# Forming the low part of every fourth weight pair with ScalarE and an accumulating transfer in an fp32 decoder trunk

## Chip, cores and metric

The kernel runs on one core of a Trainium2 chip. The metric is the device time of one execution in microseconds (us). The core's engines are TensorE (PE, with its weight loads as PEld), VectorE (DVE), ScalarE (ACT), GpSimd (POOL) and SyncE (SP); SP, ACT and POOL each have a queue from which they issue transfers to the core's 16 DMA engines.

## Reference

The kernel computes a two-layer decoder trunk in float32 for 256 positions of width 2048. Cut to what matters here:

```python
for i in range(DEPTH):                      # DEPTH = 2
    h = rms_norm(x, attn_norm_w[i])
    if i < N_A_LAYERS:
        x = x + mixer_a(h, a_w_qkv[i], a_w_o[i])
    else:
        k_blocks, v_blocks = shared_kv_blocks(x, kv_norm_w, b_w_kv, positions)
        x = x + mixer_b(h, b_w_q[j], b_w_o[j], k_blocks, v_blocks, positions)
    x = x + conv_ffn(rms_norm(x, ffn_norm_w[i]), ffn_w_up[i], ffn_conv_w[i], ffn_conv_b[i], ffn_w_down[i])
    gate = jax.nn.sigmoid(rms_norm(x, ple_norm_w[i]) @ ple_w_gate[i])
    x = x + gate * (p[i] @ ple_w_proj[i])
return rms_norm(x, final_norm_w)
```

Every `@` is a product of the 256 positions with a weight matrix of some 2048 to 11264 columns. All weights together are read once, 435 MB, and these products make up nearly all of the work.

## The kernel before

**Split operands.** TensorE multiplies in a rounded float32 format (float32r). To keep float32 accuracy, each operand is split into a high part, the value rounded to that format, and a low part, what is left: w = hi + lo. A product is then formed from three of the four partial products. For the activations the two parts stand side by side in one tile of 128 x 512 (`h`, `g`, `o` in the trace: 256 columns high, 256 low).

**The weights' way.** `weights` (L199) is a generator that feeds all large products. It walks over one strip of 512 output columns in blocks of 128 rows of the weight matrix. SyncE loads four blocks at a time (1 MB, L209) into a tile `raw`, of which there are four (`NRAW`). For each two of these blocks, a *pair*, ScalarE copies them to `whi` with rounding (L217), and VectorE subtracts, `wlo = raw - whi` (L218). There are four tiles `whi` and four `wlo` (`NWSP`), used in turn. These two instructions are issued at a raised priority (`tc.high_priority(offset=AHEAD)`), so that the scheduler puts them ahead of other work on ScalarE and VectorE as far as free buffers allow. There are 824 pairs; the first eight, while the activations are still coming in, are loaded two blocks at a time (`fine`).

**The products.** `strip_t` (L235) keeps the weights stationary: for a pair and four groups of 128 columns it issues eight matmuls with `whi` over all 512 activation columns (L246) and then eight with `wlo` over the 256 high columns (L249). `strip_1` (L252, lines L262 to L264) does the same with three shorter matmuls for each block and column group, the low one first; it serves the embedding gate and its projection. `strip_v` (L267, L276 to L278) keeps the activations stationary, for the values of the attention. `steps` (L221) sets the order of the groups: in the middle of a strip a whole pair is one group; the first pair of a strip goes output by output; the last pair (`tail=2`, in the very last strips `tail=4`: two pairs) is held back and also goes output by output, so that the four outputs become ready one after the other. The accumulators are five PSUM banks with the tag `acc`.

**Around the products.** `evac` (L281) brings an accumulator to SBUF (a ScalarE copy `c`, L283, and VectorE operations), followed in `ffn` by the convolution (L519 to L521), the gate (L531) and the split of the result (`split`, L142). The order of instructions on each engine is fixed when the program is built, by the scheduler from priorities and its own estimates; each engine then works its list in order and waits on semaphores.

Of the kernel before, what the change touches and what calls it, by code (L numbers as in the profile page):

```python
# [14 lines left out]
AF = mybir.ActivationFunctionType  # L15
OP = mybir.AluOpType
# [57 lines left out]
def tile_trunk(ctx, tc, xT_d, pT_d, pos_d, vec_d, cst_d, csb_d, wqkv, wo_a, wkv, wq_b, wo_b, wup, wdn, wpg, wpp, out_d):  # L74
    nc = tc.nc
# [9 lines left out]
    def nm(s):  # L85
        uid[0] += 1
        return f"{s}_{uid[0]}"
# [14 lines left out]
    f32 = lambda ap: ap.bitcast(F32)  # L102
# [43 lines left out]
    class Norm:  # L146
# [25 lines left out]
        def done(self, column=False):  # L172
# [23 lines left out]
            nc.vector.tensor_copy(rc[:, 0:4:2], pc[:, 0:4:2])  # L196
            return r, rc

    def weights(W, s, n, fine=False, before=lambda k0: None, base=0):  # L199

        size = 2 if fine else RAW
        for k0 in range(0, n, size):
            w = min(size, n - k0)
            raw = wraw.tile([P, RAW, 512], F32, tag="raw", name=nm("raw"))
            j = (base + k0) % W.shape[3]
            one = fine and k0 == 0
            for q in range(w) if one else (slice(0, w),):
                src = slice(j + q, j + q + 1) if one else slice(j, j + w)
                nc.sync.dma_start(raw[:, slice(q, q + 1) if one else q, :], W[s, (base + k0) // W.shape[3], :, src, :])  # L209
            for i in range(0, w, 2):  # L210
                hi = wsp.tile([P, 2, 512], F32R, tag="hi", name=nm("whi"))
                lo = wsp.tile([P, 2, 512], F32R, tag="lo", name=nm("wlo"))
                before(k0 + i)
                with tc.high_priority(offset=AHEAD):
                    for c in (slice(0, 1), slice(1, 2)) if one else (slice(0, 2),):
                        r = raw[:, i + c.start : i + c.stop]
                        nc.scalar.activation(hi[:, c], r, AF.Copy)  # L217
                        nc.vector.tensor_tensor(lo[:, c], r, f32(hi[:, c]), op=OP.subtract)  # L218
                yield k0 + i, hi, lo

    def steps(it, n, outs, tail=2, begin=True):  # L221
# [13 lines left out]
    def strip_t(W, s, xs, fine=False, before=lambda k0: None, base=0):  # L235

        n = len(xs)
        ps = [None] * 4
        for group in steps(weights(W, s, n, fine, before, base), n, 4, begin=not fine):
            if fine and group[0][0] == 0:  # L240
                group.sort(key=lambda g: g[0])
            for k, o, hi, lo in group:
                if k == 0:
                    ps[o] = bank("acc", "acc")
                c = slice(o * P, (o + 1) * P)
                nc.tensor.matmul(ps[o], hi[:, c], xs[k], start=k == 0, stop=False)  # L246
            for k, o, hi, lo in group:
                c = slice(o * P, (o + 1) * P)
                nc.tensor.matmul(ps[o][:, S:], lo[:, c], xs[k][:, :S], start=False, stop=k == n - 1)  # L249
        return ps  # L250

    def strip_1(W, s, xs, tail=2, two=None):  # L252

        n = len(xs)
        ps = [None] * 2
        a = dict(skip_group_check=True)
        for k, o, hi, lo in (g for group in steps(weights(W, s, n), n, 4, tail) for g in group):
            if k == 0 and o % 2 == 0:
                ps[o // 2] = two[:, o // 2, :] if two is not None else bank("acc", "acc")
            c = slice(o * P, (o + 1) * P)  # L260
            d = ps[o // 2][:, (o % 2) * S : (o % 2 + 1) * S]
            nc.tensor.matmul(d, lo[:, c], xs[k][:, :S], start=k == 0 and o % 2 == 0, stop=False, **a)  # L262
            nc.tensor.matmul(d, hi[:, c], xs[k][:, S:], start=False, stop=False, **a)  # L263
            nc.tensor.matmul(d, hi[:, c], xs[k][:, :S], start=False, stop=k == n - 1, **a)  # L264
        return [ps[o // 2][:, (o % 2) * S : (o % 2 + 1) * S] for o in range(4)]

    def strip_v(W, s, xs):  # L267

        n = len(xs)
        ps = [None] * 2  # L270
        for k, t, hi, lo in (g for group in steps(weights(W, s, n), n, 2) for g in group):
            if k == 0:
                ps[t] = bank("accv", "acc")
            xh = xs[k][:, t * P : (t + 1) * P]
            xl = xs[k][:, S + t * P : S + (t + 1) * P]
            nc.tensor.matmul(ps[t], xl, hi, start=k == 0, stop=False)  # L276
            nc.tensor.matmul(ps[t], xh, lo, start=False, stop=False)  # L277
            nc.tensor.matmul(ps[t], xh, hi, start=False, stop=k == n - 1)  # L278
        return ps
# [439 lines left out]
```

## Time and profile before

| what | value |
|---|---|
| median of 2 runs | 2398.07 us (2397.55 to 2398.58) |
| the profiled execution | 2398.34 us, span 2396.5 us |
| granted TensorE clock | 0.998 |
| GpSimd | 3.6 us busy, 6 instructions |
| HBM read and written | 435.55 MB and 2.10 MB, 183 GB/s over the span |
| SyncE's 1 MB weight loads | 404, median 4.8 us from issue to landing |

The span is the time from the first to the last instruction of the profiled execution. A group's row in the profile gives line, engine, operation, tile written and tiles read, shape and count; behind the bar stand the busy time, the mean duration of one in ns, the idle time just before, and what ended it. A row of waits reads "who waits <- for whom: us in total, times, longest". A row of the order of time gives the start in us, the duration, the engine and line, the operation, and in brackets the idle time before it. Several like instructions in a row are merged (x8).

### The profile page before, as it was taken

The page shows a single profiled execution, that of the slowest core. Times are in us where ns is not written, and L with a number is a line of the kernel's source. Part 1 is how long each engine was busy: PE and PEld are TensorE (multiplying, and loading weights), DVE is VectorE, ACT ScalarE, POOL GpSimd, SP SyncE. Part 2 cuts the span into 40 slices and gives each one's busy share as a digit, 9 for nine tenths or more (in the row PEclk, how much of TensorE's full clock was granted, in tenths as well). Part 3 has the DMA queues.
Part 4 walks back from the last instruction along what each step waited for, and adds up shares of the span by engine and source line. Part 5 has one row for each costly group of instructions (what it writes and reads, how often), then busy time and mean ns, then how long its engine had stood idle before and what let it go on. Part 6 is the DMA issues. An engine that isn't in the chain of part 4 may idle for free.

```text
span 2396.5 us, 35018 instructions
## 1 busy us (share of the span) xinstructions
PE 2373.7 (99%) x13914; PEld 2091.5 (87%) x13914; DVE 1651.2 (69%) x2654; ACT 1277.0 (53%) x1845; POOL 3.6 (0%) x6
## 2 busy tenths in 40 slices
PE   8999999999999999999999999999999999999997
PEld 7888888888888888888998888888888888888897
DVE  8555557777765577766778875777776557776665
ACT  6555545655643455654555444565564345565453
POOL 0000000000000000000000000000000000000000
PEclk9999999999999999999999999999999999999999
DMA  7444455555555555555455544555555555555542
GB/s 279 167 167 166 168 176 198 185 185 193 192 183 188 193 179 191 192 193 183 173 190 187 175 150 169 187 192 183 190 190 193 185 185 192 192 184 188 184 168 106
DMA packets 64004, 439.92 MB, mean 184 GB/s; under 512 B 7232, under 2 KB 7392, under 8 KB 12128
## 3 DMA queue, kind: packets, MB, share of 16 engines
q1 hardware_dynamic: 62352, 435.19, 51.6%
q8 instruction: 109, 1.79, 0.3%
q10 hardware_dynamic: 1488, 2.49, 0.3%
q14 instruction: 55, 0.45, 0.1%
HBM read 435.55 MB, written 2.10 MB: 183 GB/s over the span
## 4 chain that ended last, share of the span: by engine, by line
PE 98%; DVE 1%; ACT 0%; DMA 0%; issue 0%; DVEq 0%; SPq 0%; ACTq 0%
PE acc L246 54%; PE acc L249 27%; PE acc L264 2%; PE acc L262 2%; PE acc L263 2%; PE accv L277 2%; PE accv L276 2%; PE accv L278 2%; PE po L306 1%; PE two L262 0%; PE two L264 0%; PE two L263 0%; PE two L364 0%; PE two L448 0%; PE po L307 0%; DMA x<-in_xT 0%
## 5 line engine op out<-in xcount | busy, mean ns | idle before, releaser
L218 DVE TENSOR_TENSOR wlo<-raw,whi 128x1024 fp32r<-128x1024 f32 (+1 forms) x825 | 1008.1, 1222 | 669.3 <-ACT whi L217 662.3
L217 ACT ACTIVATE whi<-raw 128x1024 fp32r<-128x1024 f32 (+1 forms) x825 | 871.8, 1057 | 872.4 <-PE acc L246 694.9
L246 PE MATMUL acc<-h,whi 128*128 128x512 f32 x3712 | 993.3, 394 | 9.0 <-DVE h L136 9.0
L246 PEld LDWEIGHTS acc<-h,whi 128*128 128x128 f32 x3712 | 643.0, 189 | 99.3 <-DVE h L136 9.0
L249 PEld LDWEIGHTS acc<-h,wlo 128*128 128x128 f32 x3712 | 554.4, 190 | 67.9
L249 PE MATMUL acc<-h,wlo 128*128 128x256 f32 x3712 | 573.2, 282 | 0.0
L246 PE MATMUL acc<-g,whi 128*128 128x512 f32 x1408 | 369.3, 393 | 0.0
L246 PEld LDWEIGHTS acc<-g,whi 128*128 128x128 f32 x1408 | 245.7, 189 | 37.9 <-issue 1.4
L249 PEld LDWEIGHTS acc<-g,wlo 128*128 128x128 f32 x1408 | 205.2, 190 | 22.6
L249 PE MATMUL acc<-g,wlo 128*128 128x256 f32 x1408 | 210.9, 281 | 0.0
L264 PE MATMUL acc<-h,whi 128*128 128x256 f32 x512 | 145.2, 284 | 0.0
L262 PE MATMUL acc<-h,wlo 128*128 128x256 f32 x512 | 144.9, 283 | 0.0
L263 PE MATMUL acc<-h,whi 128*128 128x256 f32 x512 | 144.9, 283 | 0.0
L283 ACT ACTIVATE c<-acc 128x256 f32<-128x256 f32 x232 | 88.1, 380 | 70.4 <-PE acc L249 70.4
L246 PE MATMUL acc<-o,whi 128*128 128x512 f32 x448 | 121.3, 394 | 0.0
L264 PEld LDWEIGHTS acc<-h,whi 128*128 128x128 f32 x512 | 98.3, 192 | 0.1
L262 PEld LDWEIGHTS acc<-h,wlo 128*128 128x128 f32 x512 | 98.3, 192 | 0.1
L263 PEld LDWEIGHTS acc<-h,whi 128*128 128x128 f32 x512 | 98.3, 192 | 0.0
L284 DVE TENSOR_TENSOR c<-acc,c 128x256 f32<-128x256 f32 x232 | 96.5, 419 | 0.6
L277 PE MATMUL accv<-wlo,h 128*128 128x512 f32 x224 | 88.6, 395 | 0.0
L276 PE MATMUL accv<-whi,h 128*128 128x512 f32 x224 | 88.5, 395 | 0.0
L278 PE MATMUL accv<-whi,h 128*128 128x512 f32 x224 | 87.9, 392 | 0.0
(152 smaller groups left out, 1648.7 us busy)
## 6 DMA issues: line engine op xcount, KB each, us to landing
raw<-in_wup SPq DMA_DIRECT2D x176, 1024.0 KB, 4.8
raw<-in_wdn SPq DMA_DIRECT2D x88, 1024.0 KB, 4.8
raw<-in_wqkv SPq DMA_DIRECT2D x44, 1024.0 KB, 4.8
raw<-in_wpg SPq DMA_DIRECT2D x32, 1024.0 KB, 4.8
raw<-in_wkv SPq DMA_DIRECT2D x24, 1024.0 KB, 4.8
raw<-in_wo_a SPq DMA_DIRECT2D x16, 1024.0 KB, 4.8
raw<-in_wq_b SPq DMA_DIRECT2D x12, 1024.0 KB, 4.8
raw<-in_wo_b SPq DMA_DIRECT2D x12, 1024.0 KB, 4.8
```

What stands on the lines that cost most here:

```text
L217: nc.scalar.activation(hi[:, c], r, AF.Copy)
L218: nc.vector.tensor_tensor(lo[:, c], r, f32(hi[:, c]), op=OP.subtract)
L246: nc.tensor.matmul(ps[o], hi[:, c], xs[k], start=k == 0, stop=False)
L249: nc.tensor.matmul(ps[o][:, S:], lo[:, c], xs[k][:, :S], start=False, stop=k == n - 1)
L262: nc.tensor.matmul(d, lo[:, c], xs[k][:, :S], start=k == 0 and o % 2 == 0, stop=False, **a)
L263: nc.tensor.matmul(d, hi[:, c], xs[k][:, S:], start=False, stop=False, **a)
L264: nc.tensor.matmul(d, hi[:, c], xs[k][:, :S], start=False, stop=k == n - 1, **a)
L276: nc.tensor.matmul(ps[t], xl, hi, start=k == 0, stop=False)
L277: nc.tensor.matmul(ps[t], xh, lo, start=False, stop=False)
L278: nc.tensor.matmul(ps[t], xh, hi, start=False, stop=k == n - 1)
L283: nc.scalar.activation(c, ps[:, S:], AF.Copy)
L284: nc.vector.tensor_tensor(c, ps[:, :S], c, op=OP.add)
```

## The change

A counter numbers the pairs over the whole program. For every fourth pair outside the `fine` strip, VectorE's subtraction is left out. In its place ScalarE writes the negated high part into `wlo` (an activation with scale -1), and GpSimd issues a transfer that reads the same two blocks of the weights once more from memory and adds them to what stands in `wlo` (`accum_op=OP.add`). The sum is the same low part, w - hi. The first matmul with that `wlo` waits for the transfer's semaphore where it waited for VectorE.

```diff
+    npair = [0]
+
     def weights(W, s, n, fine=False, before=lambda k0: None, base=0):
...
                 before(k0 + i)
+                npair[0] += 1
+                by_dma = not fine and npair[0] % 4 == 0
                 with tc.high_priority(offset=AHEAD):
                     for c in (slice(0, 1), slice(1, 2)) if one else (slice(0, 2),):
                         r = raw[:, i + c.start : i + c.stop]
                         nc.scalar.activation(hi[:, c], r, AF.Copy)
-                        nc.vector.tensor_tensor(lo[:, c], r, f32(hi[:, c]), op=OP.subtract)
+                        if by_dma:
+                            nc.scalar.activation(lo, f32(hi), AF.Copy, scale=-1.0)
+                            nc.gpsimd.dma_start(
+                                lo, W[s, (base + k0) // W.shape[3], :, j + i : j + i + 2, :], accum_op=OP.add
+                            )
+                        else:
+                            nc.vector.tensor_tensor(lo[:, c], r, f32(hi[:, c]), op=OP.subtract)
```

Of the 824 pairs 204 are changed. GpSimd's list before holds no transfer. Its first rows now, after the start of the program:

```order
L224 DMA wlo_485<-in_wqkv 128x1024
L224 DMA wlo_570<-in_wqkv 128x1024
L224 DMA wlo_711<-in_wqkv 128x1024
L224 DMA wlo_780<-in_wqkv 128x1024
L224 DMA wlo_893<-in_wqkv 128x1024
```

Each of the 204 is of this form, 128 rows of 4 KB, in the order of the pairs; behind them stand the two multiplications of the end (L636 before).

On ScalarE, the start of an up strip in the first layer's FFN, before; `whi_7653` is the high part of the strip's fourth pair, the `c` belong to the strip that has just ended and `val` to its convolution:

```order
L217 ACTIVATE whi_7633<-raw_7631 128x1024
L283 ACTIVATE c_7535<-acc_7367 128x256
L283 ACTIVATE c_7548<-acc_7372 128x256
L283 ACTIVATE c_7561<-acc_7377 128x256
L519 ACTIVATE val_7533<-u_7534,vec 128x256
L217 ACTIVATE whi_7653<-raw_7631 128x1024
L519 ACTIVATE val_7546<-u_7547,vec 128x256
L283 ACTIVATE c_7574<-acc_7382 128x256
L217 ACTIVATE whi_7675<-raw_7673 128x1024
```

The same place now, where tiles have other numbers and lines stand four to ten further down:

```order
L221 ACTIVATE whi_7703<-raw_7701 128x1024
L293 ACTIVATE c_7605<-acc_7435 128x256
L293 ACTIVATE c_7618<-acc_7440 128x256
L293 ACTIVATE c_7631<-acc_7445 128x256
L529 ACTIVATE val_7603<-u_7604,vec 128x256
L221 ACTIVATE whi_7723<-raw_7701 128x1024
L529 ACTIVATE val_7616<-u_7617,vec 128x256
L223 ACTIVATE wlo_7724<-whi_7723 128x1024
L143 ACTIVATE g_7613<-val_7603 128x256
L221 ACTIVATE whi_7746<-raw_7744 128x1024
L143 ACTIVATE g_7626<-val_7616 128x256
L529 ACTIVATE val_7629<-u_7630,vec 128x256
```

The negation `wlo_7724` follows its high part with one `val` in between; of the 204 negations, 94 follow directly and 110 with one other instruction between. The fourth `c` of the old strip comes later than before. TensorE's list holds the same 13827 rows before and after, in the same order but for 34 places, in which rows change by up to 24 positions.

## The prediction

> **What bounds the kernel now.** I read the busy shares first, then the chain that ended last, then the waits. From the page, first the busy row, then the chain by engine:
>
> ```profile
> PE 2373.7 (99%) x13914; PEld 2091.5 (87%) x13914; DVE 1651.2 (69%) x2654; ACT 1277.0 (53%) x1845; POOL 3.6 (0%) x6
> PE 98%; DVE 1%; ACT 0%; DMA 0%; issue 0%; DVEq 0%; SPq 0%; ACTq 0%
> ```
>
> TensorE is busy for 2373.7 of 2396.5 us and makes up 98% of the chain. All its idle time together is 22.8 us. The waits say who is early and who is late (total us, times, longest):
>
> ```profile
> ACT whi L217 <- PE acc L246: 694.9, 504, 2.7
> DVE wlo L218 <- ACT whi L217: 662.3, 511, 5.1
> PE acc L246 <- DVE h L136: 9.0, 1, 9.0
> PEld nrm L176 <- ACT sq L165: 1.9, 2, 1.1
> ```
>
> ScalarE waits for TensorE to release a buffer of high parts, VectorE waits for ScalarE, and TensorE waits for VectorE only in the start (9.0 us), and never for a low part. The split of the weights thus runs ahead of TensorE as far as its four buffers allow, and what leaves VectorE leaves an engine that nobody waits for. The most that any relief could bring is 22.8 - 9.0 = 13.8 us, 0.6%. About 2% either way is what a measurement of this kernel can tell from no change, so the question is whether the new route of the low part is ever late for its matmul.
>
> **What moves off and on.** The two groups of the split, each kept by its shape:
>
> ```profile
> L218 DVE TENSOR_TENSOR wlo<-raw,whi 128x1024 fp32r<-128x1024 f32 x823 | 1006.7, 1223 | 662.6 <-ACT whi L217 655.6 <-PE acc L249 3.2
> L217 ACT ACTIVATE whi<-raw 128x1024 fp32r<-128x1024 f32 x823 | 870.5, 1058 | 868.3 <-PE acc L246 694.9 <-PE acc L264 64.4 <-PE accv L278 62.4
> ```
>
> 204 pairs change. VectorE loses 204 x 1.223 = 249 us, worth nothing by the waits above. ScalarE gains 204 copies of the same size; taking the 1.058 us of the first copy, that is 216 us, and its share goes from 53% to 62%. Its 694.9 us of waiting for TensorE cover that; without this cover each would cost 1.06 us, 216 us in all. The PE order is the same but for a few places of up to 24 rows, which I cost at nothing: most of the work in them is independent, and where it is not, at the matmul of a norm, the wait shown above is about 1 us. On POOL only other transfers of this kind stand behind a waiting one, 11 us apart, so a wait there delays nobody else; on ScalarE the high part of the next pair stands behind the negation, due 2.8 us later than it; on TensorE everything stands behind the low matmul.
>
> **The time that the transfer has.** There are four buffers of low parts, and every fourth pair is changed, so a changed pair always gets the buffer of the changed pair before. It may be negated when that pair's last low matmul ends, and must be complete at its own first low matmul. An up strip has eight pairs, and the changed ones are its fourth and its last. From the order of time, the last pair of one strip:
>
> ```profile
> 837.17 1.12 PE L249 MATMUL acc<-h,wlo 128*128 128x256 f32 x8
> 837.37 1.06 ACT L217 ACTIVATE whi<-raw 128x1024 fp32r<-128x1024 f32 x1 [0.74 <-PE acc L246]
> 846.97 0.39 PE L249 MATMUL acc<-h,wlo 128*128 128x256 f32 x2
> ```
>
> The buffer is free at 837.17 + 1.12 = 838.29, the high part stands at 838.43, a negation of 1.06 would end at 839.49, and the first low matmul comes at 846.97: 7.5 us for the transfer, its issue and its semaphores. The fourth pair of the next strip takes over that buffer:
>
> ```profile
> 849.06 0.40 PE L249 MATMUL acc<-h,wlo 128*128 128x256 f32 x2
> 849.57 1.05 ACT L217 ACTIVATE whi<-raw 128x1024 fp32r<-128x1024 f32 x1
> 850.51 0.59 ACT L519 ACTIVATE val<-u,vec 128x256 f32<-128x256 f32 x1
> 859.50 1.11 PE L249 MATMUL acc<-h,wlo 128*128 128x256 f32 x8
> ```
>
> Here the new order puts L529 of the changed kernel (the L519 above, 0.59) ahead of the negation: it ends near 851.10 + 1.06 = 852.16, and 7.3 us are left. In the middle of a strip no such boundary shortens the time:
>
> ```profile
> 812.24 1.06 ACT L217 ACTIVATE whi<-raw 128x1024 fp32r<-128x1024 f32 x1 [1.73 <-PE acc L246]
> 823.22 1.12 PE L249 MATMUL acc<-h,wlo 128*128 128x256 f32 x8
> ```
>
> The pair copied at 812.24 has its low matmuls four pairs on, at 823.22: 823.22 - 812.24 - 2 x 1.06 = 8.9 us. By their places in the program, 118 of the 172 changed pairs of this kind (the strips of L249) are at a boundary, with about 7.4, and 54 have about 8.8. The strips of L262, with 18 changed pairs, use the low part first of all:
>
> ```profile
> 1151.53 0.28 PE L262 MATMUL acc<-h,wlo 128*128 128x256 f32 x1
> 1152.09 1.06 ACT L217 ACTIVATE whi<-raw 128x1024 fp32r<-128x1024 f32 x1 [1.00 <-PE acc L264]
> 1160.53 0.28 PE L262 MATMUL acc<-h,wlo 128*128 128x256 f32 x1
> ```
>
> The high part stands at 1153.15, the negation would end at 1154.21, and the use is at 1160.53: 6.3 us. The last strip holds back four blocks, and there the buffer comes free late; the last two rows are a value strip's:
>
> ```profile
> 2360.71 0.28 PE L262 MATMUL two<-p,wlo 128*128 128x256 f32 x1
> 2365.75 0.28 PE L262 MATMUL acc<-h,wlo 128*128 128x256 f32 x1
> 2368.83 1.06 ACT L217 ACTIVATE whi<-raw 128x1024 fp32r<-128x1024 f32 x1 [1.82 <-PE acc L264]
> 2375.11 0.28 PE L262 MATMUL acc<-h,wlo 128*128 128x256 f32 x1
> 72.58 1.06 ACT L217 ACTIVATE whi<-raw 128x1024 fp32r<-128x1024 f32 x1 [0.49 <-PE accv L278]
> 81.86 0.39 PE L277 MATMUL accv<-wlo,h 128*128 128x512 f32 x1
> ```
>
> 2365.75 - (2360.71 + 0.28 + 1.06) = 3.7 us; the next changed pair has 2375.11 - 2368.83 - 2.12 = 4.2. A value strip has 81.86 - 72.58 - 2.12 = 7.2, and there are 14 such pairs. A transfer of length L costs TensorE L minus this time, each time, since a stall shifts the next release and the next use alike.
>
> **How long the transfer takes.** No row of before shows an accumulating transfer or one that GpSimd issues. The nearest are SyncE's loads (KB each, median us from issue to landing) and their queue:
>
> ```profile
> raw<-in_wup SPq DMA_DIRECT2D x176, 1024.0 KB, 4.8
> raw<-in_wpp SPq DMA_DIRECT2D x8, 512.0 KB, 3.5
> q1 hardware_dynamic: 62352, 435.19, 51.6%
> raw<-in_wqkv SPq DMA_DIRECT2D x7, 512.0 KB, 6.8
> ```
>
> The lower end is the plain load of its size, 3.5 us: under every time above but none short of it, so it costs nothing. The upper end is twice a load of 1 MB, 9.6 us. Between them: an addition into SBUF must read 512 KB of weights and 512 KB of the negated part, as much reading as a 1 MB load, so I take 4.8. A weight load is under way at the same time: the raw buffer of a changed pair is now released by ScalarE's copy, not by VectorE 1.2 us later, so SyncE issues the next load about 1.1 us ahead of the transfer. A packet takes 0.516 x 16 x 2396.5 / 62352 = 0.317 us of an engine, and 1 MB is 8 rows of 8 KB on each engine, 2.5 us. Half of that in the way is 1.25 us. With 0.35 for GpSimd's semaphore and issue, L = 6.4 us, nearer to the 6.8 of the crowded loads of the start than to either end. The 204 transfers read 214 MB by this count, 214/435 of what the weights take, and the 16 engines rise from 51.6% by 25% to 77%: not full. Raw loads may be late by 2.5 us; their four buffers cover eight pairs of 2.8 us, and without that cover it would be 2.5 us per load.
>
> The Trainium skill ("DMA: Bandwidth & Descriptors", Anatomy of one DMA) gives about 2.0 us plus bytes over 436 GB/s for a GpSimd-issued transfer; by it 512 KB would be an estimated 3.2 us, and the sum would be that of the lower end, which no run here shows. The same skill ("Collectives: The Full Stack", the bandwidth ceiling) says that a reducing transfer runs at half the rate because it reads two sources, and not because of the addition; by it the addition would cost nothing beyond the second read, and I would give the case of a too long transfer 0.25 in place of the 0.40 below. No run here shows it yet.
>
> The sum at 6.4: L249 strips 0; L262 strips 16 x 0.1 = 1.6; the last two 2.7 + 2.2 = 4.9; value strips 0. Together 6.5, say 7 us. The span becomes 2403.5. The profiled execution took 2398.34 us with a span of 2396.5, 1.8 around it, and lies 0.3 above the median of 2398.07: the time is 2405 us.
>
> **Rivals.** *The transfer is too long for its buffer (slower).* The place is TensorE's first low matmul of a changed pair, which then waits for the transfer. It decides from L = 7.6 on, where 118 x 0.2 + 18 x 1.3 + the value strips make some 50 us, 2%. At the upper end of 9.6 it costs 118 x 2.2 + 54 x 0.8 + 18 x 3.4 + 14 x 2 = 392 us: 2790. For it: only 1.2 us lie between my L and the point, and the addition and GpSimd's start are unmeasured. Against it: the reads are bounded by rows, and the loads of the same moment land in 4.8.
>
> *GpSimd's descriptors wait for VectorE.* If each issue must wait for one VectorE instruction, 1.22 us by the row above, L is 7.6 and the time about 2398 + 50 = 2448, on the border. VectorE is busy 69% of the time, so a part would wait. The Trainium skill ("SBUF — State Buffer", Who interferes with whom) has such a lock for two-port copies, and says tensor_tensor does not hold GpSimd's writes; by that rule this rival falls, and no run here shows it.
>
> *Relief.* TensorE's idle time shrinks with a freer VectorE: at best 13.8 us, 2384. For it there is only the 22.8 us of idle time; against it that almost none of it is put down to L218.
>
> **How the numbers follow.** Forecast (L up to 7.6, 2394 to 2446): 0.48. Too long: 0.40. Descriptors: 0.06, half on either side of 2%. Relief: 0.06, of which 0.01 is over 2% by something that I do not see. So faster 0.01, same 0.48 + 0.03 + 0.05 = 0.56, slower 0.43. The likeliest one's own range is 2394 to 2446. The range for 8 in 10 leaves out the rest of the relief below and a transfer of over 9.4 us above: 2394 to 2760.
>
> **What would show it.** Right: no TensorE wait for wlo beyond the strips of L262, transfers landing in about 6 us, ScalarE near 1493 us and VectorE near 1402, DMA near 77%. A landing over 7.6 us, and a wait of TensorE for the accumulated wlo some 200 times in the list of waits, would make it wrong; a longer span without that wait would mean that another mechanism is at work.

## The result, and the profile after

The changed kernel takes 2435.4 us, the median of two runs (2431.13 and 2439.68), against 2398.07 before: a ratio of 1.0156, with a 95% interval of 1.0139 to 1.0174. It is slower by 37 us, 1.6%, where 7 us were forecast. The interval lies well clear of 1, so a measurement of this kernel can tell a smaller change than the 2% that the prediction named. The profiled execution took 2431.13 us with a span of 2428.9, which is 32.4 us more than the span before.

From the page of the changed kernel, first the busy row, the chain by engine and the two queues of weight traffic (packets, MB, share of the 16 engines):

```profile
PE 2383.2 (98%) x13914; PEld 2090.8 (86%) x13914; DVE 1428.1 (59%) x2450; ACT 1461.5 (60%) x2049; POOL 180.0 (7%) x210
PE 88%; DMA 8%; ACT 2%; issue 1%; DVE 0%; DVEq 0%; SPq 0%; ACTq 0%
q1 hardware_dynamic: 62352, 435.19, 52.3%
q0 software_dynamic: 29376, 106.97, 24.0%
```

VectorE lost 223 us, ScalarE gained 185, and the DMA engines rose to 52.3 + 24.0 = 76%: nothing is full but TensorE. TensorE's idle time rose from 22.8 to 2428.9 - 2383.2 = 45.7 us and its busy time by 9.5. The chain now goes through DMA for 8% of the span. That share is not the loss: 8% is 194 us, and where a transfer takes the place of the matmuls that ran beside it, the chain loses only what the transfer lasts longer than they do.

TensorE's waits for a DMA, from the list of waits (total us, times, longest), which had no such line before:

```profile
PE acc L259 <- DMA wlo<-in_wup: 11.8, 12, 1.8
PE acc L272 <- DMA wlo<-in_wpg: 4.3, 6, 1.4
PE accv L287 <- DMA wlo<-in_wkv: 3.2, 3, 1.6
PE two L272 <- DMA wlo<-in_wpp: 2.2, 1, 2.2
PE acc L259 <- DMA wlo<-in_wdn: 1.1, 2, 0.8
```

They make 22.6 us, nearly the whole rise of the idle time (22.9), and all end at the first matmul with an accumulated low part. (L259, L272 and L287 are the L249, L262 and L277 of before.) The list holds 24 stalls of some size. Set side by side by the program's order, 54 of the 204 transfers land less than 0.3 us before their first matmul. Call the time from the start of one matmul to the start of the next a step: the 54 steps that end at these matmuls are together 28.4 us longer than the same steps in the trace of before, and all steps together are 32.3 us longer, as the span is.

The transfers themselves, first from the list of DMA issues (KB each, median us from issue to landing), then the answer for the line that issues them, over all 204:

```profile
raw<-in_wup SPq DMA_DIRECT2D x176, 1024.0 KB, 4.9
wlo<-in_wup POOLq DMA_DIRECT2D x88, 512.0 KB, 6.2
wlo<-in_wpg POOLq DMA_DIRECT2D x16, 512.0 KB, 5.7
```

```profile
DMA to landing us min/median/max: 5.3/6.5/8.9
L224 POOL DMA_DIRECT2D wlo<-in_wup x88: 862/862/888, 404.4 to 2181.9; - x88
```

A transfer lands 6.5 us after its issue in the median, but anywhere from 5.3 to 8.9. GpSimd's instruction takes 0.862 us nearly every time, and it starts 0.29 us after the end of the negation in the median (in three of the 204 it starts 1.0 to 2.3 us after).

One late transfer in the order of time (start, duration, engine, line; in brackets the idle time ahead and what ended it):

```profile
1769.04 1.06 ACT L221 ACTIVATE whi<-raw 128x1024 fp32r<-128x1024 f32 x1 [1.24 <-PE acc L256]
1770.31 1.04 ACT L223 ACTIVATE wlo<-whi 128x1024 fp32r<-128x1024 f32 x1
1771.65 0.86 POOL L224 DMA_DIRECT2D wlo<-in_wup  x1 [9.09 <-ACT wlo L223]
1778.17 0.63 PE L256 MATMUL acc<-h,whi 128*128 128x512 f32 x2
1780.56 0.51 PE L259 MATMUL acc<-h,wlo 128*128 128x256 f32 x2 [1.75 <-DMA wlo<-in_wup]
```

And one that is just in time, at another strip's end:

```profile
838.78 1.04 ACT L223 ACTIVATE wlo<-whi 128x1024 fp32r<-128x1024 f32 x1
840.12 0.86 POOL L224 DMA_DIRECT2D wlo<-in_wup  x1 [9.10 <-ACT wlo L223]
847.11 0.44 PE L259 MATMUL acc<-h,wlo 128*128 128x256 f32 x2
```

From the end of the negation to the first low matmul the second has 847.11 - 839.82 = 7.3 us; that is the time left at a boundary. In the first the same stretch is 1780.56 - 1771.35 = 9.2. In both, SyncE's next raw load was issued about 1.5 us ahead of the transfer:

```profile
1770.12 0.33 SPq L211 DMA_DIRECT2D raw<-in_wup  x1
```

The reason follows from the program: the changed pair is the second of its raw block, so ScalarE's copy of it (ended at 1770.10) releases that block, and the load of the next 1 MB starts there; the negation and the transfer come after it.

### The profile page after: what moved, and what is told of

Its sections match the earlier page's. It is cut to its first block, busy times and chain, and to the rows that moved or that the text cites. A ratio compares the mean times of both kernels' runs of the same rounds, so it can differ in the third digit from the quotient of the medians.

```text
span 2428.9 us, 35365 instructions
## 1 busy us (share of the span) xinstructions
PE 2383.2 (98%) x13914; PEld 2090.8 (86%) x13914; DVE 1428.1 (59%) x2450; ACT 1461.5 (60%) x2049; POOL 180.0 (7%) x210
## 3 DMA queue, kind: packets, MB, share of 16 engines
q1 hardware_dynamic: 62352, 435.19, 52.3%
## 4 chain that ended last, share of the span: by engine, by line
PE 88%; DMA 8%; ACT 2%; issue 1%; DVE 0%; DVEq 0%; SPq 0%; ACTq 0%
PE acc L256 49%; PE acc L259 25%; DMA wlo<-in_wup 4%; PE acc L272 2%; PE accv L287 2%; PE accv L288 2%; PE acc L274 2%; PE acc L273 2%; PE accv L286 2%; DMA wlo<-in_wpg 2%; ACT wlo L223 1%; DMA wlo<-in_wkv 1%; ACT whi L221 1%; DMA wlo<-in_wdn 1%; PE po L316 1%
## 5 line engine op out<-in xcount | busy, mean ns | idle before, releaser
L228 DVE TENSOR_TENSOR wlo<-raw,whi 128x1024 fp32r<-128x1024 f32 (+1 forms) x621 | 759.0, 1223 | 804.3 <-ACT whi L221 795.5
L259 PEld LDWEIGHTS acc<-h,wlo 128*128 128x128 f32 x3712 | 552.0, 190 | 88.5 <-DMA wlo<-in_wup 21.0
L259 PE MATMUL acc<-h,wlo 128*128 128x256 f32 x3712 | 574.5, 282 | 12.2 <-DMA wlo<-in_wup 11.8
L259 PEld LDWEIGHTS acc<-g,wlo 128*128 128x128 f32 x1408 | 204.8, 190 | 25.2 <-DMA wlo<-in_wdn 3.1
L223 ACT ACTIVATE wlo<-whi 128x1024 fp32r<-128x1024 f32 x204 | 214.9, 1053 | 3.4 <-PE acc L259 0.5
L259 PE MATMUL acc<-g,wlo 128*128 128x256 f32 x1408 | 211.5, 282 | 1.1 <-DMA wlo<-in_wdn 1.1
L272 PE MATMUL acc<-h,wlo 128*128 128x256 f32 x512 | 145.8, 285 | 4.3 <-DMA wlo<-in_wpg 4.3
L224 POOL DMA_DIRECT2D wlo<-in_wup x88 | 76.0, 863 | 923.2 <-ACT wlo L223 576.2
L272 PEld LDWEIGHTS acc<-h,wlo 128*128 128x128 f32 x512 | 98.2, 192 | 5.5 <-DMA wlo<-in_wpg 5.5
L287 PE MATMUL accv<-wlo,h 128*128 128x512 f32 x224 | 88.8, 397 | 3.2 <-DMA wlo<-in_wkv 3.2
```

What stands on the lines that cost most here:

```text
L223: nc.scalar.activation(lo, f32(hi), AF.Copy, scale=-1.0)
L224: nc.gpsimd.dma_start(lo, W[s, (base + k0) // W.shape[3], :, j + i : j + i + 2, :], accum_op=OP.add)
```

## The experiments

Each edit is against the changed kernel. The kernel before took 2397.6 to 2397.8 us on the same chips; ratios are to it.

**neg_only: no transfer.**

```diff
-                            nc.gpsimd.dma_start(
-                                lo, W[...], accum_op=OP.add
-                            )
```

> The changed kernel without its 204 transfers: ScalarE still writes the negated high part, and the low matmuls use that (left out: the addition of the weights). If the loss is TensorE's wait for transfers, as I hold, the time falls back to before, 2397 to 2402 us, and no low matmul waits. If ScalarE's 215 us of added copies and the other order on it (evacuations and gates later) make the loss, it stays near 2430. If the extra traffic of the transfers slows something else, it also falls back, so this run alone doesn't tell wait from traffic.

It took 2395.81 us, 0.9992 (0.9983 to 1.0001), with no wait of TensorE for a low part. So the moved work of ScalarE and VectorE and the new order cost nothing, and the relief of VectorE is worth 0.2% at the most. The whole loss hangs on the transfer.

**traffic_no_wait: the same transfers, but nobody reads them.** VectorE forms the low part as before; the negation and the transfer go to a tile of their own (another tile gave up a buffer for it).

```diff
-                            nc.scalar.activation(lo, f32(hi), AF.Copy, scale=-1.0)
-                            nc.gpsimd.dma_start(lo, W[...], accum_op=OP.add)
+                            nc.vector.tensor_tensor(lo[:, c], r, f32(hi[:, c]), op=OP.subtract)
+                            sc = wsp.tile([P, 2, 512], F32R, tag="scr", bufs=1, name=nm("scr"))
+                            nc.scalar.activation(sc, f32(hi), AF.Copy, scale=-1.0)
+                            nc.gpsimd.dma_start(sc, W[...], accum_op=OP.add)
```

> VectorE forms every low part as before, and for every fourth pair ScalarE and GpSimd do the negation and the accumulating transfer into a tile that nobody reads (one such tile; the two buffers of the attention's weights are reduced to one to make room). All the work and traffic of the change and more is there, only TensorE's wait for it is not. Wait theory: 2398 to 2406 us. Traffic theory (the loads of raw weights come late, or the memories are contended): 2420 us or more, with TensorE waiting for raw or for VectorE. The transfers' landing should stay near 6.5 us in the median.

It took 2398.07 us, 1.0002 (0.9992 to 1.0012): the traffic, and GpSimd's work for it, cost nothing as long as no matmul waits. The landing was not as expected. From its list of issues:

```profile
raw<-in_wup SPq DMA_DIRECT2D x176, 1024.0 KB, 5.8
scr<-in_wup POOLq DMA_DIRECT2D x88, 512.0 KB, 7.9
```

VectorE reads the raw block again, so the next load is issued 1.2 us later, now only 0.1 us ahead of the transfer (median of the 204), and both are longer: 7.9 us in place of 6.2, 5.8 in place of 4.9. In the changed kernel itself the 89 transfers with a raw load 1.0 to 1.45 us ahead land in 6.9 us in the median, the 70 with one 1.6 to 2.5 us ahead in 5.8. The farther a raw load is ahead, the sooner the transfer lands.

**plain_transfer: a copy without the addition.** The negation is left out too.

```diff
-                            nc.scalar.activation(lo, f32(hi), AF.Copy, scale=-1.0)
-                                lo, W[...], accum_op=OP.add
+                                lo, W[...]
```

> GpSimd's transfer copies the weights into the low tile without adding, and the negation is left out (the low part is then the weight itself). One read in place of two: packets of 4096 bytes should take about 160 ns, not 328, so the data take 1.3 us less, and landing falls from 6.5 to about 5.2 us in the median. Without the negation another 1.06 us are gained. Wait theory: almost no transfer is late, 2397 to 2403 us. If the time of a transfer were set by GpSimd's issue and not by the reads, landing would stay at 6 us or more.

It took 2400.93 us, 1.0014 (1.0004 to 1.0023). Its page has

```profile
L223 POOL DMA_DIRECT2D wlo<-in_wup x88 | 46.4, 528 | 937.1 <-PE acc L258 937.1
q0 software_dynamic: 29376, 106.97, 14.7%
```

so the time is as expected, and no matmul waits for a transfer (landing 5.5 us in the median over the 204, where 5.2 was expected). Without the negation a transfer also has more time, so this run does not tell shorter transfers from more time. The same number of bytes takes 14.7% of the engines where the accumulating one took 24.0%, and the issue takes 0.53 us, not 0.86. By packets, one of 4096 bytes takes 174 ns plain and 328 ns accumulating (medians of 26112 each).

**five_low_buffers: a fifth low buffer, so that the negation need not wait for the pair four back** (the tile `w` gives up a buffer for it).

```diff
-                lo = wsp.tile([P, 2, 512], F32R, tag="lo", name=nm("wlo"))
+                lo = wsp.tile([P, 2, 512], F32R, tag="lo", bufs=5, name=nm("wlo"))
```

> The change as it is, with five buffers of low parts in place of four (the two buffers of the attention's weights are reduced to one to make room). Each transfer gets one pair, 2.8 us, more. Wait theory: 8.9 us of landing at most, plus 0.3, stay under 7.4 + 2.8 everywhere but perhaps at the very end: 2397 to 2404 us. If the transfers' landing stays near 6.5 us while the time falls back, only the time that they have matters. Theory that ScalarE's order makes the loss: near 2430.

It took 2431.47 us, 1.0142 (1.0127 to 1.0157), and the longest group of waits is still there:

```profile
PE acc L259 <- DMA wlo<-in_wup: 12.1, 13, 1.7
```

The expectation failed. The negation reads the high part, whose four buffers set its time: in before, the low buffer came free after the high copy's end in at most 2 of the 204 changed pairs. A buffer buys time only on the tile that is released last. **fourth_again**, the changed kernel unaltered in a later group of runs, took 2430.66 us (2428.87 to 2440.88), 1.0149 (1.0124 to 1.0173).

> The changed kernel again, beside its three siblings that change another pair of every four. Its changed pairs are the second of their 1 MB load (their high copy releases the raw buffer, and the next load is issued 1.4 us ahead of the transfer), and the time that a transfer has is short (median 7.8 us by the trace of before, counted from the end of the negation). Expected: 2430 to 2440 us, landing 6.5 us in the median with a tail to 9.

**first_pair, second_pair, third_pair: which pair of four is changed.** The first and the third are the first pair of a raw block, the second and the fourth the second pair of one.

```diff
-                by_dma = not fine and npair[0] % 4 == 0
+                by_dma = not fine and npair[0] % 4 == 1     # 2, 3
```

> The first of every four pairs is changed in place of the fourth: first of its load, so the next load is issued after the second pair's split, some 3 us later; the time for a transfer is as short as for the fourth (median 7.5 us by the trace of before). Collision theory: landing about 5.4 to 5.8 us in the median, few late, 2399 to 2407 us. Theory that two reads and GpSimd's start alone make the 6.5 us: landing and time as for the fourth, 2430 or more.

> The second of every four pairs: second of its load, as the fourth is, but in the middle of the strips, where a transfer has 8.8 us. Collision theory: landing as for the fourth, 6.5 us in the median with a tail to 9, but late only in the gate strips and in the tail: 2404 to 2414 us. If landing alone decided, and not the time that is left, it would be 2430 as for the fourth.

> The third of every four pairs: first of its load and in the middle of the strips, 8.8 us. Both effects are gone: landing 5.4 to 5.8 us, 2397 to 2402 us, no gain beyond 10 us over before, since TensorE was idle for 22.8 us only.

The places in the raw blocks hold outside the strips of L272. There each block of `wpp` is a single pair, which shifts the count: in third_pair 8 of the 18 changed pairs of these strips have a raw load only 1.4 us ahead, as a second pair has.

The three took 2433.1 (1.0146, 1.0131 to 1.0161), 2422.37 (1.0103, 1.0088 to 1.0118) and 2414.44 us (1.007, 1.0055 to 1.0085), all longer than expected. The landings followed the raw load as expected: with a lead of 2.9 us, 5.3 and 5.5 us in the median for first_pair and third_pair; with 1.4 us, 6.5 for second_pair. But few late transfers were enough. The waits of first_pair, then of third_pair:

```profile
PE acc L272 <- DMA wlo<-in_wpg: 6.6, 8, 2.2
PE two L272 <- DMA wlo<-in_wpp: 5.2, 2, 3.2
PE acc L259 <- DMA wlo<-in_wup: 4.3, 2, 2.2
PE acc L259 <- DMA wlo<-in_wqkv: 3.3, 1, 3.3
PE acc L259 <- DMA wlo<-in_wkv: 2.5, 1, 2.5
```

```profile
PE two L272 <- DMA wlo<-in_wpp: 5.0, 2, 4.0
PE acc L272 <- DMA wlo<-in_wpg: 4.6, 5, 1.8
```

All waits of third_pair lie in the strips of L272 (the gate and two blocks of `wpp`), which use the low part first. Of its eight transfers that land less than 0.3 us before their matmul seven are among these 8: there the collision that the third pair was to avoid was back. In second_pair, too, 13 of the 20 transfers that land so late lie in these strips. In first_pair four long stalls in other strips come on top, and a loss that the list of waits does not show, told at the end. Why just those four were late was not tried.

**fourth_not_gate, third_not_gate: the same two places, without the strips of L272** (186 transfers; VectorE forms the low parts there).

```diff
-    def weights(W, s, n, fine=False, before=lambda k0: None, base=0):
+    def weights(W, s, n, fine=False, before=lambda k0: None, base=0, late=True):
-                by_dma = not fine and npair[0] % 4 == 0
+                by_dma = late and not fine and npair[0] % 4 == 0     # 3
-        for k, o, hi, lo in (g for group in steps(weights(W, s, n), n, 4, tail) for g in group):
+        for k, o, hi, lo in (g for group in steps(weights(W, s, n, late=False), n, 4, tail) for g in group):
```

> The change without the strips of L262 to L264 (the embedding gate and its projection), which form all low parts on VectorE: 186 transfers. By the first uses of the changed kernel, these strips hold about 9 of the 33 us that are lost and the others 24: 2419 to 2424 us. If most of the loss hung on the gate strips, where a transfer has least time: under 2410.

> The third pair of every four, and not in the gate strips: 186 transfers that are first of their load and have 8.8 us or more. In the run of the third pair nearly all late first uses were in the gate strips. So nothing is left: 2395 to 2400 us, and landing 5.5 us in the median. If something else in the change costs time, over 2403.

They took 2421.75 us (1.0098, 1.0078 to 1.0118) and 2399.87 (1.0008, 0.9999 to 1.0018), both as expected. In fourth_not_gate the waits of the ordinary strips stay; third_not_gate has one wait left, and its landings are short:

```profile
PE acc L259 <- DMA wlo<-in_wup: 8.4, 13, 1.6
```

```profile
PE accv L287 <- DMA wlo<-in_wkv: 1.0, 1, 1.0
```

```profile
DMA to landing us min/median/max: 5.2/5.5/7.8
```

Of the changed kernel's 33 to 37 us, 9 to 14 thus belong to the strips of L272, and 24 to the other strips.

**five_high_and_low: a fifth buffer of high and of low parts, and one raw buffer less.**

```diff
-NRING, NRAW, NWSP = 42, 4, 4
+NRING, NRAW, NWSP = 42, 3, 5
```

> The change with five buffers of high parts and five of low parts; to make room, three buffers of raw weights in place of four. Five low buffers alone changed nothing, and I put that down to the negation: it reads the high part, which has four buffers and so can be written no earlier. With five of both, every transfer gets 2.8 us more. If that is so and TensorE's wait is the loss: 2397 to 2403 us, with landing as before at 6.4 us in the median. If the wait does not depend on the buffers, or if three raw buffers are too few: 2425 or more.

It took 2398.95 us, 1.0007 (0.9998 to 1.0017), with no wait of TensorE for a transfer, although these landed no sooner:

```profile
DMA to landing us min/median/max: 5.3/6.8/9.6
```

So the loss is what a transfer takes above the time that it has: more time alone takes the loss away. That shorter landings alone would do so is not shown. third_not_gate has both, short landings and the longer time in the middle of the strips; first_pair, with short landings in the median and the short time, lost 35 us. Neither of the two runs without a loss beats the kernel before.

**every_second: twice the transfers, 408.**

```diff
-                by_dma = not fine and npair[0] % 4 == 0
+                by_dma = not fine and npair[0] % 2 == 0
```

> Every second pair is changed, all of them second of their load: 408 transfers. If the transfers' losses add up one by one, the losses of the second and of the fourth pair together, 25 + 33 us: 2450 to 2460 us. By the busy shares the 16 engines would then stand at 52 + 2 x 24 = 100%; if that makes each transfer wait for the one before, landing rises over 8 us and the time is over 2520 us.

It took 2606.64 us, 1.0855 (1.0809 to 1.0901). Its queues, and the two longest lines of its waits:

```profile
q1 hardware_dynamic: 62352, 435.19, 47.3%
q0 software_dynamic: 58752, 213.94, 44.7%
```

```profile
PE acc L259 <- DMA wlo<-in_wup: 61.1, 60, 3.7
PE acc L259 <- DMA wlo<-in_wdn: 40.2, 28, 3.9
```

With 92% of the DMA engines busy the loss grows about sixfold for twice the transfers. This was the branch of saturation in the expectation, and not the one of a loss per transfer, though the median landing (7.6 us) stayed a little under what that branch named. That the full engines make the landing longer was not separated from the other effects of twice the transfers.

## Why the prediction came out as it did

**What bounds the kernel: right.** TensorE still does, and what left VectorE and came to ScalarE was worth nothing in either direction (neg_only within 0.2%; traffic_no_wait the same time as before). ScalarE's 1493 and VectorE's 1402 us were off by 2%, the DMA share of 77% by one point. The raw loads land in 4.9 us, as before (4.8), and TensorE waits for none of them.

**The place: right.** The loss is at TensorE's first low matmul of a changed pair, where the rival of a too long transfer was put, and the time left at a boundary, 7.3 to 7.5 us, was right: in neg_only, where no transfer follows, 114 of the 172 changed pairs of the L249 strips have 7.3 to 7.5 us from the end of the negation to their first low matmul. But the sign that the prediction named for being right, no wait for a low part beyond the strips of L262, did not come: 17 of the 24 waits listed lie in other strips.

**The length of the transfer: right in the median.** L was 6.4 us; from the negation's end to the landing it measures 6.75. The trace's packet records show that its terms erred in opposite directions, so that the closeness is in part luck. No row stood behind the 0.35 us for GpSimd's semaphore and issue. GpSimd's issue starts 0.29 us after the negation, and the first data packet comes 1.6 us after that with the raw load far ahead (third_pair), where SyncE's loads of before need 0.96: about 0.9 us more than a SyncE load in all. The load in the way, put at 1.25, adds 1.0 (first packet 2.6 us after the issue in the changed kernel). From the first packet to the landing it is 3.9 us, as much as for the 1 MB load of 4.8 us (3.8). An accumulating packet takes about twice the time: a plain 4096-byte packet took 159 ns in the kernel before, 174 in plain_transfer, and 328 accumulating. The Trainium skill ("Collectives: The Full Stack", the bandwidth ceiling) has the halved rate come from the two sources and not from the addition. The packets agree with the halved rate; no run here tells the second read from the addition. The Trainium skill's 2.0 us plus bytes over 436 GB/s ("DMA: Bandwidth & Descriptors", Anatomy of one DMA), by estimate 3.2 us here, is near the shortest plain transfer (3.5 us), while the shortest accumulating one of all runs took 5.1 (first_pair).

**The step that failed: "L249 strips 0".** One length was set against one time left, 6.4 against 7.4, and the difference taken as nothing lost. But a wait costs what is above the time left, and nothing is given back below it; the sum takes the tail of the lengths, and not their middle. From the negation's end to the landing the 204 transfers measured 5.6 to 9.2 us. 47 of them took over 7.4, and the mean excess over 7.4, counted over all, is 0.116 us: for the 118 pairs at a boundary that is 13.7 us, where the median gives 0. Measured were 42 late transfers in these strips and 17.3 us. Taken pair by pair, each transfer's length in the changed kernel against the time that the same pair has in neg_only, the excess adds up to 15.8 us in these strips and 26.8 in all, of the 28.4 that the late steps lost. One stretch at half clock adds up to 1.7, and about 2 us lie elsewhere. The spread could have been seen coming: half of a raw load's 2.5 us "in the way" was itself a mean over loads in the way fully or not at all, and with it the lengths would have gone up to 4.8 + 2.5 + 0.35 = 7.65.

**The two other terms.** The strips of L272 with the end were put at 1.6 + 4.9 = 6.5 and measured 7.4 by the steps (9 to 14 by the runs without them), but that agreement is luck. Of the "last two" only the very last was late, by 1.5 us in place of 2.2; the other, put at 2.7, had 6.2 us in neg_only and lost nothing. The 3.7 us given to it rested on the pair four back still holding its buffer, and a row of before contradicts that: its low part was written from 2358.30 on, while the pair four back was read until 2360.99.

```profile
2358.30 1.23 DVE L218 TENSOR_TENSOR wlo<-raw,whi 128x1024 fp32r<-128x1024 f32 x1
```

The other 5.9 us came from the remaining pairs of these strips, put at 1.6: six of their transfers took 6.5 to 8.6 us against 6.1 to 6.3 left, while their median was 6.0: again the spread and not the median. The value strips were put at 0, with 7.2 us left and 6.4 needed, and measured 3.7: the time left was taken from one pair, while seven of the 14 had 6.0 to 7.0 us in neg_only, and in three of these the transfer took 7.7 to 7.9.

**How far it was luck.** The time fell inside the range of 2394 to 2446 us because the range had been drawn up to the point where the same rival costs 50 us; the sum itself had a fifth of the loss that came.

**The rivals.** The point of decision, "from L = 7.6 on", was reckoned with a single L too; the transfers that passed it did cost. *Descriptors that wait for VectorE* were not seen: GpSimd starts 0.29 us after the negation in the median and takes 0.862 us, as much for the 166 issues that overlap an instruction of VectorE as for the others, and third_not_gate lands in 5.5 us beside a VectorE that is as busy (60% against 59%). *Relief* is at most what neg_only shows.

**What stays open.** Why, at the same lead of 1.5 us, the second of the two transfers shown above lands in 6.9 us and the first in 8.9. The DMA engines are no fuller in the stretch of the late one. Their stretches (start and end, length, busy time with instructions of PE, PEld, DVE, ACT and POOL, granted clock, DMA share, GB/s):

```profile
836.00:850.00 14.00, 14.00 (x82) 12.19 (x81) 7.29 (x11) 7.54 (x12) 0.86 (x1) 1.00 0.83 258
1768.00:1782.00 14.00, 12.25 (x71) 10.52 (x70) 5.57 (x8) 6.09 (x8) 0.86 (x1) 1.00 0.81 253
```

Transfers with a packet of instruction loading within 2 us of them were longer in the median (6.8 us for 101 against 6.1 for 103), which was only counted and not tried. By the packet records most of the spread lies between the first packet and the last, 2.8 to 6.0 us.

## What to carry to other kernels

When the time that a buffer leaves to a transfer is close to the transfer's length, set the spread of the length against it and not the median: the expected loss is the mean of what lies above the time left, times the number of transfers, and a stall is not paid back. Look then at what else is issued in the same microsecond: moving the transfer to the other pair of a raw block, so that a 1 MB load was 2.9 us ahead of it and not 1.4, shortened it by 1 us. And ask first whether anybody waits for the engine that is relieved; here even a transfer that is never late gained nothing.

## What the runs showed of the hardware

The length of an accumulating 512 KB transfer follows the lead of the 1 MB load ahead of it: with 0.1 us (traffic_no_wait) 7.9 us, with 1.4 to 1.5 (the changed kernel) 6.5, with 2.9 (third_pair) 5.5; all medians. The packet records show where the time goes: from the start of the issue to the first data packet 4.5, 2.6 and 1.6 us in these three runs, and from there to the last packet 3.2, 3.5 and 3.6. The lead is not all: at 1.5 us, but with 92% of the DMA engines busy, it was 7.6 (every_second).

After some stalls TensorE's clock is halved for a while, so that they cost more than themselves (read from the clock records, and not tried by itself). TensorE stands still for 2.2 us in the changed kernel, until 1246.6, and then has this row among the stretches of 14 to 16 us (columns as above):

```profile
1240.00:1256.00 16.00, 13.75 (x88) 12.87 (x87) 8.98 (x17) 9.24 (x15) 0.86 (x1) 0.89 0.69 209
```

The mean clock of 0.89 is one stretch of 3.41 us at half clock in the trace's clock records, so up to 1.7 us lost (half its length). First_pair, with fewer but longer stalls, has six such stretches of 3.4 to 6.8 us (one of them in its start) before the one at its end, up to 12 us lost, and so a lower mean clock over its whole span than the 0.998 of before:

```profile
core 0: 2431.7 us, clock 0.993
```

That, beside 21.9 us of waits, is nearly all of its 35 us. In every_second 24 such stretches cost up to 43 us. There was no sharp bound: in first_pair an idle gap of 1.98 us (until 1174.1) was followed by one, and a gap of 2.23 us (until 446.2) was not. The Trainium skill ("TensorE: Matmul & The Clock Gate", Part 1) gives a free-running window of about 3.4 us and an idle one after which the clock is halved; the length of the stretches agrees with that, but here stalls shorter than the window were enough.
